# Attention scores: own PSUM banks and an own minimum for each component, and six banks in rotation ahead of attention

## The chip, the cores and the metric

The kernel runs on one core of one Trainium2 chip. The metric is the device time of one execution in microseconds, the median of three runs. [...]

## What is computed

One step of a hybrid trunk: a gated feed-forward half step, then a mixer of two branches (differential attention and a bidirectional mLSTM) whose outputs are gated by sigmoids and summed, then a second half step. 512 sample tokens and 128 prompt tokens are laid out as 640 columns. The part that matters here is the attention: 8 heads, each with two components c of 64 features, whose softmaxes are subtracted.

```python
s = einsum('bqhcd,bkhcd->bhcqk', q, k) * scale
pr = softmax(s, axis=-1)
w = pr[:, :, 0] - lam * pr[:, :, 1]
out = einsum('bhqk,bkhv->bqhv', w, v)
```

The stage ahead of it computes twelve 256-column slices of the input projection (`w_gd`, `w_gm`, `w_mo`, `w_mq`, `w_mk`), the branch gates among them.

## The kernel before

All matrix products are fp32 made of three products of a high part (`H`) and a low part (`L`); splitting a weight takes a copy on ScalarE (the high part) and a subtraction on VectorE (the low part). TensorE's instructions stand in the order in which the code is written. Those of ScalarE and VectorE are ordered by the framework's scheduler, except where the code pins them, so a change of what waits for what can move them.

The stages in time: FFN1 up to 466 us; from there to 505 us the second half of norm2, the projections of q and k of the first two heads (`tok_group`, L1220: two or three units of 128 tokens at a time, 8 steps k of 3 matmuls for each unit, then an evacuation by ScalarE into `q_tok` or `k_tok`) and the gate products `ps_g`; the gate items (`class Gates`, L1783, run by `Winograd.products`, L383 to L453) from 505 to 655 us; the preparation of head 0; attention from 684 to 1070 us; then mLSTM, the output and FFN2.

A gate item is one 1024 x 256 slice of weights in a Winograd scheme of seven products, each of 12 matmuls over 320 columns. It takes three PSUM tiles X, Y, Z (`acc_tile`, names `ps_f` in the profile). TensorE's order for item i is: A11 into X; ScalarE copies X to Y; S1 into Z; then the tail of item i-1 (A22 into its Y); S2 into Y, copied to SBUF as `u2` by ScalarE; the rest of the tail (S4 into the Z of item i-1, read by `done(1, 0, Z, u2)`); A12 into X, read by `done(0, 0, X, None)`; S3 into Y, copied as `u3`, and Z with u3 is read by `done(1, 1, Z, u3)`. A `done` writes a tile `g_out`, by VectorE where it adds a `u`, and stores it. Beside that ScalarE and VectorE split the weights of the coming items (`wB`, `wC` by `parts`, the sums `ww` by `sums`), and in items 1 to 5 they also normalise and rotate q and k (`rope`, `ss`, `q_tok`, `k_tok`). From item 5 on, VectorE also computes columns of the modulation (`junk,mod<-raw_a,csil`).

In attention each head has four blocks of 128 sample tokens with 768 keys and one block of 128 prompt tokens with 128 keys. Per block: `scores` (L1597) writes both components into one tile `sc` of three banks, VectorE takes the minimum of both (L1617; q is scaled by a negative number), `soft` makes the exponents of each component on ScalarE with that minimum as bias, `mix` combines them on VectorE, `turn` transposes the weights (`ps_wT`, copied to `wT` by ScalarE), and `values` multiplies by v (`ps_o`). Between these, `fill` puts matmuls of other projections (`ps_t`, `ps_p`), so that TensorE has work while the chain runs. All tiles but `sc` rotate through the five banks of the pool `ps2`, in the order in which the code asks for them.

```python
for c in range(2):
    if qi < 4:
        for k0, k1 in (((0, 512), (512, 768)) if c == 0 else ((0, 256), (256, 768))):
            o = s[:, c * 768 + k0 : c * 768 + k1]
...
placed(vec.tensor_reduce(out=mn, in_=sv, axis=AX.X, op=ALU.min))
```

Of the kernel before, what the change touches and what calls it, by code (L numbers as in the profile page):

```python
# [31 lines left out]
def tile_trunk(ctx: ExitStack, tc: tile.TileContext, a: dict):  # L32
# [4 lines left out]
    def placed(ins):  # L37
        if as_written[0] is in_row:
            i = ins.ins
            if i.engine in in_row:  # L40
                tc.add_manual_dep(
                    i, in_row[i.engine].name, mybir.DependencyInfo(mybir.DependencyClass.NoSync, mybir.DependencyReason.DATA),
                    reason="written",
                )
            in_row[i.engine] = i
        elif as_written[0]:
            tc.keep_in_program_order(ins)
        return ins

    def act(*args, **kw):  # L50
        return placed(nc.scalar.activation(*args, **kw))  # L51
# [22 lines left out]
    def mm(*args, **kw):  # L74
        tc.keep_in_program_order(nc.tensor.matmul(*args, **kw))  # L75
# [88 lines left out]
    class Banks:  # L164


        def __init__(self, pool):
            self.pool, self.order = pool, list(range(8))

        def tile(self, shape, dtype, tag, name):  # L170
            i = self.order.pop(0)
            self.order.append(i)
            return self.pool.tile(shape, dtype, tag=f"b{i}", name=name)
# [657 lines left out]
    with ExitStack() as ph:  # L831
# [514 lines left out]

    att = ExitStack()
    qk = att.enter_context(tc.tile_pool(name="qk", bufs=1))
    psum = att.enter_context(tc.tile_pool(name="ps2", bufs=5, space=PSUM))
    ps_s = att.enter_context(tc.tile_pool(name="ps2s", bufs=1, space=PSUM))  # L1350

    fill = Fill()


    def gate_products():
        raw = load(rawp, [128, KT, 128], a["w_g"], tag="raw", name="wg_raw")
        wgH = wide_p.tile([128, KT, 128], F32R, tag="BH", name="wgH", bufs=2)
        wgL = wide_p.tile([128, KT, 128], F32R, tag="BL", name="wgL", bufs=2)
        act(wgH, raw, AF.Copy)
        tt(vec, wgL, raw, wgH.bitcast(F32), ALU.subtract)  # L1360
        ps = ps_s.tile([128, 1536], F32, tag="sc", name="ps_g")

        def step(hf, k):
            cs = half(hf)
            mm3(ps[:, 512 * hf : 512 * hf + HALF], wgH[:, k, :], wgL[:, k, :], hH[:, k, cs], hL[:, k, cs], k == 0, k == KT - 1)

        return ps, step
# [175 lines left out]
    class Head:  # L1543
# [51 lines left out]
                self.turn_features(self.kp2, self.kL, True, lambda o, i: act(o, i, AF.Copy))  # L1595

        def scores(self, qi):  # L1597
            s = ps_s.tile([128, 1536], F32, tag="sc", name="sc")
            qs = slice(qi * 128, (qi + 1) * 128)
            qT, kH, kL = self.qT, self.kH, self.kL  # L1600
            for c in range(2):
                if qi < 4:
                    for k0, k1 in (((0, 512), (512, 768)) if c == 0 else ((0, 256), (256, 768))):
                        o = s[:, c * 768 + k0 : c * 768 + k1]
                        mm(o, qT[:, c, qs], kH[:, c, k0:k1], start=True, stop=False)
                        mm(o, qT[:, c, qs], kL[:, c, k0:k1], start=False, stop=True)
                else:

                    o = s[:, c * 512 : c * 512 + 256].rearrange("p (c t) -> p c t", c=2)
                    mm(o, qT[:, c, qs], kH[:, :, 768:896], start=True, stop=False)  # L1610
                    mm(o, qT[:, c, qs], kL[:, :, 768:896], start=False, stop=True)
            if qi < 4:
                sv = s.rearrange("p (c t) -> p c t", c=2)
            else:
                sv = s[:, 0:1280].rearrange("p (c t) -> p c t", c=2)[:, :, 0:128]
            mn, sm, rc = (ap.tile([128, 2], F32, tag=n, name=n, bufs=2) for n in ("mn", "sm", "rc"))
            placed(vec.tensor_reduce(out=mn, in_=sv, axis=AX.X, op=ALU.min))  # L1617
            self.s[qi] = sv, 768 if qi < 4 else 128, mn, sm, rc

        def soft(self, qi):  # L1620
            sv, w, mn, sm, rc = self.s[qi]
            p0 = ap.tile([128, 768], F32, tag="p0", name="p0", bufs=2)
            p1 = ap.tile([128, 768], F32, tag="p1", name="p1")
            for c, p in enumerate((p0, p1)):
                self.exp = act(p[:, :w], sv[:, c, :], AF.Exp, bias=mn[:, c : c + 1], scale=-1.0, accum_out=sm[:, c : c + 1])
            self.s[qi] = p0, p1, w, sm, rc

        def mix(self, qi):
# [201 lines left out]
    ropes, tabs, nlam, gs, rope_p = [], [], [None], [None], [None]  # L1830
    wide = ExitStack()
    wide_p = wide.enter_context(tc.tile_pool(name="wide", bufs=1))
    G = Gates(wide_p, ntmp, psum)

    (src_q, e_q), (src_k, e_k) = project_q(0, ropes.append), project_k(0, ropes.append)
    e_q, e_k = e_q(), e_k()
# [4 lines left out]

    def norm2_second(k):
        if k == 2:
            box["normed"] = norm2(psum, 1)

    tok_group(psum, [(w_q, 0, e_q), (w_q, 1, e_q)], norm2_second)
    tok_group(psum, [(w_k, 0, e_k), (w_k, 1, e_k)], lambda k: None)
    with tc.issue_after(box["normed"]):
        ps_g, gate_step = gate_products()

    heads = [Head(hd) for hd in range(8)]
    gates = ExitStack()
    tok_group(psum, [(w_q, i, e_q) for i in (2, 3, 4)], lambda k: None)
    G.work[0][0].load()
    with tc.issue_after(box["normed"]):
        third, fourth = G.operand_sums(lambda r: box["x"][1][:, 2 * r : 2 * r + 2, :])
        third()
        fourth()
    x_stack.close()
    tok_group(psum, [(w_k, i, e_k) for i in (2, 3, 4)], lambda k: None)  # L1860
    for k in range(KT):
        for hf in range(2):
            gate_step(hf, k)
# [702 lines left out]
```

## Time and profile before

| | us |
|---|---|
| median of 3 runs | 1814.83 (1814.38 to 1815.23) |
| profiled execution, its own time | 1815.7 |
| its span | 1813.9 |
| TensorE busy | 1785.6 (98%) |
| VectorE busy | 1349.6 (74%) |
| ScalarE busy | 910.8 (50%) |
| 466 to 505 us: TensorE busy | 37.6 of 39 |
| 505 to 655 us: TensorE busy | 148.4 of 150 |
| 655 to 684 us: TensorE busy | 29.0 of 29 |
| 684 to 1070 us: TensorE busy | 380.9 of 386 |

PE is TensorE's matmuls, PEld its weight loads, DVE VectorE, ACT ScalarE. In a row of the timeline the first number is the start in us from the span's start, the second the duration; then the engine, the line, the operation, the output and inputs by their names, the shapes, and in brackets the idle time ahead of it with what ended it. In a row of the waits stand the waiting engine and tile, what ended the wait, the total in us, the count and the longest. In a row of the windows stand, after the length, the busy time (and number of instructions) of PE, PEld, DVE, ACT and POOL, the granted clock, the DMA share and GB/s. L75 is the matmul helper, L51 the activation helper, L54 `tensor_tensor`, L57 `scalar_tensor_tensor`, L61 `tensor_scalar`: the tile's name tells which one it is.

### The profile page before, as it was taken

The page shows a single profiled execution, that of the slowest core. Times are in us where ns is not written, and L with a number is a line of the kernel's source. Part 1 is how long each engine was busy: PE and PEld are TensorE (multiplying, and loading weights), DVE is VectorE, ACT ScalarE, POOL GpSimd, SP SyncE. Part 2 cuts the span into 40 slices and gives each one's busy share as a digit, 9 for nine tenths or more (in the row PEclk, how much of TensorE's full clock was granted, in tenths as well). Part 3 has the DMA queues.
Part 4 walks back from the last instruction along what each step waited for, and adds up shares of the span by engine and source line. Part 5 has one row for each costly group of instructions (what it writes and reads, how often), then busy time and mean ns, then how long its engine had stood idle before and what let it go on. Part 6 is the DMA issues. An engine that isn't in the chain of part 4 may idle for free.

```text
span 1813.9 us, 30780 instructions
## 1 busy us (share of the span) xinstructions
PE 1785.6 (98%) x12550; PEld 1744.6 (96%) x12550; DVE 1349.6 (74%) x2178; ACT 910.8 (50%) x1588; POOL 39.2 (2%) x69
## 2 busy tenths in 40 slices
PE   8999999999999999999999999999999999999998
PEld 6999999999999999999999998899999999999998
DVE  6879987677888765858584557977767888897485
ACT  5654544333655445556564547674336545554432
POOL 0000000100000000000000000000000000000010
PEclk9999999999999999999999999999999999999999
DMA  8355566977245434221221124576642355557992
GB/s 326 111 198 171 186 236 221 350 227 266 83 139 181 160 131 143 78 69 63 69 69 55 68 81 163 182 257 218 221 171 80 134 173 185 203 180 274 353 311 80
DMA packets 132207, 311.36 MB, mean 172 GB/s; under 512 B 10017, under 2 KB 93217, under 8 KB 119009
## 3 DMA queue, kind: packets, MB, share of 16 engines
q1 hardware_dynamic: 121122, 265.22, 42.3%
q0 software_dynamic: 10256, 41.55, 7.1%
q8 instruction: 98, 1.61, 0.4%
q10 hardware_dynamic: 688, 2.63, 0.4%
q14 instruction: 43, 0.35, 0.1%
HBM read 240.49 MB, written 68.87 MB: 171 GB/s over the span
## 4 chain that ended last, share of the span: by engine, by line
PE 85%; DVE 7%; DMA 4%; ACT 2%; issue 1%; SPq 0%; DVEq 0%; ACTq 0%
PE ps_f L75 48%; PE ps_p L75 14%; PE ps_t L75 12%; PE sc L75 2%; PE ps_n L75 2%; PE ps_o L75 2%; DVE ww L54 2%; PE ps_u L75 1%; DMA raw_a<-in_w_ada_k 1%; PE ps_wT L78 1%; PE ps_qkT L78 1%; DMA raw<-in_w2b 1%; DVE junk L814 1%; DMA P<-nm_dram 1%; DVE mn L1617 1%
## 5 line engine op out<-in xcount | busy, mean ns | idle before, releaser
L75 PE MATMUL ps_f<-S,ww 128*128 128x320 f32 x2400 | 387.5, 310 | 5.2 <-DVE ww L54 1.9
L75 PEld LDWEIGHTS ps_f<-S,ww 128*128 128x128 f32 x2400 | 359.8, 188 | 9.6 <-DVE ww L54 6.5
L54 DVE TENSOR_TENSOR ww<-raw,ww 128x2048 fp32r<-128x2048 f32 (+1 forms) x73 | 163.9, 2246 | 74.3 <-ACT ww L51 74.2
L75 PE MATMUL ps_t<-wH,hH 128*128 128x256 f32 x640 | 185.7, 290 | 0.9 <-DVE x L57 0.9
L75 PE MATMUL ps_f<-hm,ww 128*128 128x320 f32 x1176 | 185.8, 309 | 0.1
L75 PE MATMUL ps_t<-wH,hL 128*128 128x256 f32 x640 | 181.6, 284 | 0.9 <-DVE hL L54 0.9
L75 PE MATMUL ps_t<-wL,hH 128*128 128x256 f32 x640 | 181.4, 283 | 0.0
L75 PEld LDWEIGHTS ps_f<-hm,ww 128*128 128x128 f32 x1176 | 175.7, 188 | 0.6 <-DVE ww L54 0.6
L51 ACT ACTIVATE ww<-raw 128x2048 fp32r<-128x2048 f32 (+1 forms) x73 | 136.9, 1875 | 60.3 <-DVE raw L54 33.0
L54 DVE TENSOR_TENSOR raw<-raw 128x1024 f32<-128x1024 f32 x186 | 161.0, 865 | 2.2
L75 PE MATMUL ps_f<-hm,wB 128*128 128x320 f32 x1008 | 161.5, 309 | 0.0
L75 PE MATMUL ps_p<-hH,wH 128*128 128x320 f32 x480 | 151.1, 315 | 0.7 <-ACT aT L51 0.7
L75 PEld LDWEIGHTS ps_f<-hm,wB 128*128 128x128 f32 x1008 | 151.3, 188 | 0.0
L75 PE MATMUL ps_p<-hH,wL 128*128 128x320 f32 x480 | 148.3, 309 | 0.0
L75 PE MATMUL ps_p<-hL,wH 128*128 128x320 f32 x480 | 148.3, 309 | 0.0
L51 ACT ACTIVATE u<-ps_f 128x320 f32<-128x320 f32 x129 | 55.8, 433 | 161.5 <-PE ps_f L75 159.7
L75 PEld LDWEIGHTS ps_t<-wH,hH 128*128 128x128 f32 x640 | 123.0, 192 | 1.5 <-ACT nsq L51 1.1
L75 PEld LDWEIGHTS ps_t<-wH,hL 128*128 128x128 f32 x640 | 122.9, 192 | 1.1 <-DVE hL L54 1.1
L75 PEld LDWEIGHTS ps_t<-wL,hH 128*128 128x128 f32 x640 | 123.1, 192 | 0.4
L1617 DVE TENSOR_REDUCE mn<-sc 128x2 f32<-128x1536 f32 (+1 forms) x40 | 59.5, 1489 | 56.0 <-PE sc L75 55.8
L54 DVE TENSOR_TENSOR wB<-raw,wB 128x1024 fp32r<-128x1024 f32 x64 | 78.1, 1221 | 26.7 <-ACT wB L51 26.7
L51 ACT ACTIVATE wH<-raw 128x2048 fp32r<-128x2048 f32 (+1 forms) x45 | 75.4, 1681 | 42.2 <-PE ps_p L75 35.5
(309 smaller groups left out, 3621.9 us busy)
## 6 DMA issues: line engine op xcount, KB each, us to landing
g_dram<-g SPq DMA_DIRECT2D x44, 640.0 KB, 7.6
raw_a<-in_w_ada_c POOLq DMA_DIRECT2D x35, 512.0 KB, 4.7
g_dram<-g SPq DMA_DIRECT2D x24, 480.0 KB, 8.1
raw<-in_w1b SPq DMA_DIRECT2D x11, 1024.0 KB, 4.9
raw<-in_w3b SPq DMA_DIRECT2D x11, 1024.0 KB, 6.3
raw<-in_w1a SPq DMA_DIRECT2D x10, 1024.0 KB, 4.9
raw<-in_w3a SPq DMA_DIRECT2D x10, 1024.0 KB, 6.2
hm<-g_dram SPq DMA_DIRECT2D x7, 1280.0 KB, 12.5
```

Of the source, the lines that this page charges most:

```text
L51: return placed(nc.scalar.activation(*args, **kw))
L54: return placed(eng.tensor_tensor(out=out, in0=in0, in1=in1, op=op))
L75: tc.keep_in_program_order(nc.tensor.matmul(*args, **kw))
L78: tc.keep_in_program_order(nc.tensor.transpose(*args, **kw))
L814: placed(vec.tensor_tensor_reduce(out=junk, in0=raw, in1=self.csil[:, v, :], op0=ALU.mult, op1=ALU.add, scale=1.0, scalar=0.0, accum_out=m ...
L1617: placed(vec.tensor_reduce(out=mn, in_=sv, axis=AX.X, op=ALU.min))
```

## The change

The ring `ps2` has four banks instead of five. The score tiles become two, tags `s0` and `s1`, of two banks each. In `scores` every component has its own tile, the larger piece (512 keys) always first, and its own minimum over 768 (or 128) columns; the exponent of a component reads that tile and that column of `mn`. Ahead of attention the two banks of `s1` serve as a fifth and sixth bank: the class `Six` hands out tiles in turn, four from the ring and then the two halves of one tile `more`. The projections `tok_group`, the second half of norm2 and the gate items take their tiles from it. `ps_g` lies in `s0`.

```diff
-    psum = att.enter_context(tc.tile_pool(name="ps2", bufs=5, space=PSUM))
+    psum = att.enter_context(tc.tile_pool(name="ps2", bufs=4, space=PSUM))
     ps_s = att.enter_context(tc.tile_pool(name="ps2s", bufs=1, space=PSUM))
+
+    class Six:
+
+
+        def __init__(self):
+            self.n, self.more = 0, ps_s.tile([128, 1024], F32, tag="s1", name="more")
+
+        def tile(self, shape, dtype, tag, name):
+            n, self.n = self.n % 6, self.n + 1
+            return psum.tile(shape, dtype, tag=tag, name=name) if n < 4 else self.more[:, 512 * n - 2048 : 512 * n - 1536]
+
+    six = Six()
...
-        ps = ps_s.tile([128, 1536], F32, tag="sc", name="ps_g")
+        ps = ps_s.tile([128, 1024], F32, tag="s0", name="ps_g")
...
         def scores(self, qi):
-            s = ps_s.tile([128, 1536], F32, tag="sc", name="sc")
             qs = slice(qi * 128, (qi + 1) * 128)
             qT, kH, kL = self.qT, self.kH, self.kL
+            mn, sm, rc = (ap.tile([128, 2], F32, tag=n, name=n, bufs=2) for n in ("mn", "sm", "rc"))
+            sv = []
             for c in range(2):
+                s = ps_s.tile([128, 1024], F32, tag=f"s{c}", name="sc")
                 if qi < 4:
-                    for k0, k1 in (((0, 512), (512, 768)) if c == 0 else ((0, 256), (256, 768))):
-                        o = s[:, c * 768 + k0 : c * 768 + k1]
-                        mm(o, qT[:, c, qs], kH[:, c, k0:k1], start=True, stop=False)
-                        mm(o, qT[:, c, qs], kL[:, c, k0:k1], start=False, stop=True)
+                    for k0, k1 in ((0, 512), (512, 768)):
+                        mm(s[:, k0:k1], qT[:, c, qs], kH[:, c, k0:k1], start=True, stop=False)
+                        mm(s[:, k0:k1], qT[:, c, qs], kL[:, c, k0:k1], start=False, stop=True)
+                    sv.append(s[:, 0:768])
                 else:
...
-            placed(vec.tensor_reduce(out=mn, in_=sv, axis=AX.X, op=ALU.min))
+                    sv.append(s[:, 128 * c : 128 * c + 128])
+                placed(vec.tensor_reduce(out=mn[:, c : c + 1], in_=sv[c], axis=AX.X, op=ALU.min))
...
-                self.exp = act(p[:, :w], sv[:, c, :], AF.Exp, bias=mn[:, c : c + 1], scale=-1.0, accum_out=sm[:, c : c + 1])
+                self.exp = act(p[:, :w], sv[c], AF.Exp, bias=mn[:, c : c + 1], scale=-1.0, accum_out=sm[:, c : c + 1])
...
-    G = Gates(wide_p, ntmp, psum)
+    G = Gates(wide_p, ntmp, six)
...
-    tok_group(psum, [(w_k, 0, e_k), (w_k, 1, e_k)], lambda k: None)
+    tok_group(six, [(w_k, 0, e_k), (w_k, 1, e_k)], lambda k: None)
...
-    tok_group(psum, [(w_q, i, e_q) for i in (2, 3, 4)], lambda k: None)
+    tok_group(six, [(w_q, i, e_q) for i in (2, 3, 4)], lambda k: None)
```

Besides the 40 reductions more on VectorE the instructions are the same, and TensorE has them in the same order. What they wait for differs, and ScalarE and VectorE are ordered anew. Three places follow.

TensorE at the end of item 1 and the start of item 2 of the gate items, with the engines that a row waits for. The rows `<-S,ww` are S3 of item 1, the rows `<-hH,wB` the first product A11 of item 2, written into its tile X. Before:

```order
L75 MATMUL ps_f<-S,ww 128x320 [waits Activation_49]
L75 MATMUL ps_f<-S,ww 128x320 x11
L75 MATMUL ps_f<-hH,wB 128x320
L75 MATMUL ps_f<-hL,wB 128x320
L75 MATMUL ps_f<-hH,wB 128x320 x2
```

The same place in the changed program, where X is the second half of `more`:

```order
L75 MATMUL ps_f<-S,ww 128x320 [waits Activation_49]
L75 MATMUL ps_f<-S,ww 128x320 x11
L75 MATMUL more<-hH,wB 128x320 [waits DVE_49]
L75 MATMUL more<-hL,wB 128x320
L75 MATMUL more<-hH,wB 128x320 x2
```

No matmul has moved; the first into `more` waits for VectorE, where no wait stood before. The instruction it waits for is the `g_out` that reads the Z of item 1 in the other half of `more`.

ScalarE in item 8 of the gate items, from the copy of X to Y (`ps_f<-ps_f`, then `ps_f<-more`) to the weight parts `wC`. `ww<-raw` is the high part of the weight sums of item 9, `g_out` an evacuation, `u` the copy u2. Before:

```order
L51 ACTIVATE ps_f<-ps_f 128x320
L51 ACTIVATE g_out<-ps_f 128x320
L51 ACTIVATE ww<-raw 128x2048
L51 ACTIVATE u<-ps_f 128x320
L51 ACTIVATE wC<-raw 128x512
```

The changed program:

```order
L51 ACTIVATE ps_f<-more 128x320
L51 ACTIVATE ww<-raw 128x2048
L51 ACTIVATE g_out<-ps_f 128x320
L51 ACTIVATE u<-ps_f 128x320
L51 ACTIVATE wC<-raw 128x512
```

`ww<-raw` has moved ahead of the evacuation `g_out`, which it followed.

VectorE in item 5 and at the start of item 6. `ww<-raw,ww` is the low part of the weight sums of item 6, `junk,mod` the modulation column, and the last row the `g_out` that reads the Z of item 5 with u3. Before:

```order
L54 TENSOR_TENSOR g_out<-ps_f,u 128x320
L54 TENSOR_TENSOR raw<-raw 128x4x128
L61 TENSOR_SCALAR g_out<-g_out 128x320
L814 ISA junk,mod<-raw_a,csil 128x1024
L814 ISA mod 128x1
L54 TENSOR_TENSOR ww<-raw,ww 128x2048
L54 TENSOR_TENSOR wB<-raw,wB 128x1024
L54 TENSOR_TENSOR wC<-raw,wC 128x512
L814 ISA junk,mod<-raw_a,csil 128x1024
L814 ISA mod 128x1
L57 SCALAR_TENSOR_TENSOR g_out<-ps_f,u 128x320
```

The changed program:

```order
L54 TENSOR_TENSOR ww<-raw,ww 128x2048
L54 TENSOR_TENSOR g_out<-ps_f,u 128x320
L814 ISA junk,mod<-raw_a,csil 128x1024
L814 ISA mod 128x1
L54 TENSOR_TENSOR wC<-raw,wC 128x512
L61 TENSOR_SCALAR g_out<-g_out 128x320
L814 ISA junk,mod<-raw_a,csil 128x1024
L814 ISA mod 128x1
L54 TENSOR_TENSOR wB<-raw,wB 128x1024
L57 SCALAR_TENSOR_TENSOR g_out<-more,u 128x320
```

`ww` now stands ahead of the first `junk,mod`, which it followed; the last `g_out` still comes after both `junk,mod` and the two weight parts.

More of the change, by code (lines that the diff above doesn't have):

```diff
@@ L1597, in scores @@
         def scores(self, qi):
-            s = ps_s.tile([128, 1536], F32, tag="sc", name="sc")
             qs = slice(qi * 128, (qi + 1) * 128)
             qT, kH, kL = self.qT, self.kH, self.kL
+            mn, sm, rc = (ap.tile([128, 2], F32, tag=n, name=n, bufs=2) for n in ("mn", "sm", "rc"))
+            sv = []
             for c in range(2):
+                s = ps_s.tile([128, 1024], F32, tag=f"s{c}", name="sc")
                 if qi < 4:
-                    for k0, k1 in (((0, 512), (512, 768)) if c == 0 else ((0, 256), (256, 768))):
-                        o = s[:, c * 768 + k0 : c * 768 + k1]
-                        mm(o, qT[:, c, qs], kH[:, c, k0:k1], start=True, stop=False)
-                        mm(o, qT[:, c, qs], kL[:, c, k0:k1], start=False, stop=True)
+                    for k0, k1 in ((0, 512), (512, 768)):
+                        mm(s[:, k0:k1], qT[:, c, qs], kH[:, c, k0:k1], start=True, stop=False)
+                        mm(s[:, k0:k1], qT[:, c, qs], kL[:, c, k0:k1], start=False, stop=True)
+                    sv.append(s[:, 0:768])
                 else:
-                    o = s[:, c * 512 : c * 512 + 256].rearrange("p (c t) -> p c t", c=2)
+                    o = s[:, 0:256].rearrange("p (c t) -> p c t", c=2)
                     mm(o, qT[:, c, qs], kH[:, :, 768:896], start=True, stop=False)
                     mm(o, qT[:, c, qs], kL[:, :, 768:896], start=False, stop=True)
[L1612 to L1617, printed above, removed]
+                    sv.append(s[:, 128 * c : 128 * c + 128])
+                placed(vec.tensor_reduce(out=mn[:, c : c + 1], in_=sv[c], axis=AX.X, op=ALU.min))
             self.s[qi] = sv, 768 if qi < 4 else 128, mn, sm, rc
@@ L1843, in norm2_second @@
         if k == 2:
-            box["normed"] = norm2(psum, 1)
-    tok_group(psum, [(w_q, 0, e_q), (w_q, 1, e_q)], norm2_second)
-    tok_group(psum, [(w_k, 0, e_k), (w_k, 1, e_k)], lambda k: None)
+            box["normed"] = norm2(six, 1)
+    tok_group(six, [(w_q, 0, e_q), (w_q, 1, e_q)], norm2_second)
+    tok_group(six, [(w_k, 0, e_k), (w_k, 1, e_k)], lambda k: None)
     with tc.issue_after(box["normed"]):
@@ L1859, in tile_trunk @@
     x_stack.close()
-    tok_group(psum, [(w_k, i, e_k) for i in (2, 3, 4)], lambda k: None)
+    tok_group(six, [(w_k, i, e_k) for i in (2, 3, 4)], lambda k: None)
     for k in range(KT):
```

## The prediction

> **What bounds the kernel now.** The page comes first: of 1813.9 us TensorE is busy for 1785.6, so a change can give back little and has to be judged by which waits of TensorE it takes away and which it adds.
>
> ```profile
> span 1813.9 us, 30780 instructions
> PE 1785.6 (98%) x12550; PEld 1744.6 (96%) x12550; DVE 1349.6 (74%) x2178; ACT 910.8 (50%) x1588; POOL 39.2 (2%) x69
> ```
>
> Then the busy time by stage, over the three stretches that the change touches: the first token projections with the second half of norm2, the twelve gate items, and attention.
>
> ```profile
> 466.00:505.00 39.00, 37.56 (x291) 36.52 (x292) 36.09 (x57) 25.53 (x48) 0.00 (x0) 1.00 0.20 67
> 505.00:655.00 150.00, 148.36 (x1012) 148.09 (x1011) 115.73 (x158) 73.56 (x113) 2.11 (x4) 1.00 0.49 167
> 684.00:1070.00 386.00, 380.85 (x3034) 370.82 (x3033) 250.91 (x385) 214.90 (x453) 0.00 (x0) 1.00 0.22 74
> ```
>
> The first number after each length is TensorE's busy time: it stands still for 1.4, 1.6 and 5.2 us. VectorE is full in the first stretch (36.1 of 39) and at 77% in the second. The waits of TensorE over 466 to 1070 us say what ends that idle time:
>
> ```profile
> PE ps_wT L78 <- DVE p L57: 3.0, 7, 0.8
> PE ps_f L75 <- DVE ww L54: 1.6, 1, 1.6
> PE sc L75 <- ACT p L51: 1.6, 3, 0.9
> PE ps_t L75 <- DVE hL L54: 0.9, 1, 0.9
> PE ps_o L75 <- ACT wT L51: 0.5, 1, 0.5
> ```
>
> The columns are the total, the count and the longest. In attention only three lines belong to the chain scores, minimum, exponent, mix, turn: 5.1 us in all. That is the most a shorter chain could give back.
>
> **The change part by part.**
>
> *The chain in attention.* Per block one reduction over both components becomes two over one each, and the exponent of component 0 no longer waits for component 1.
>
> ```profile
> L75 PE MATMUL sc<-kH,qT x144: 274/283/500, 683.8 to 1063.5; 128*128 128x256 f32 x80, 128*128 128x512 f32 x64
> L51 ACT ACTIVATE p<-sc,mn x80: 366/896/923, 687.9 to 1065.5; 128x768 f32<-128x768 f32 x64, 128x128 f32<-128x128 f32 x16
> L1617 DVE TENSOR_REDUCE mn<-sc x40: 417/1758/1760, 686.1 to 1063.9; 128x2 f32<-128x1536 f32 x32, 128x2 f32<-128x256 f32 x8
> ```
>
> From 417 ns at 256 columns and 1758 at 1536 a column costs 1.048 ns and the rest 149 ns; 768 columns are then 0.95 us (an estimate), two of them 1.91 against 1.76. VectorE gets 0.15 us more for each of 32 blocks, 4.8 us in all, in a stretch where it is idle for 135 of 386: I cost this at nothing. The first exponent starts about 1.5 us earlier (0.8 of the reduction, 0.7 of component 1's four matmuls: five gate products of 12 matmuls over 320 columns take 8.80 us, below, so 256 columns take 0.12 and 512 twice that; an estimate). Of the 5.1 us I take the three waits of scores on the exponents whole (1.6 us) and 0.9 of the 3.5 in front of the turn and the values: most of those follow VectorE's weight splits and ScalarE's rope copies, which stay. Gain 2.5 us, between 1 and 4.
>
> *Four banks instead of five in attention.* Every tile of the ring now needs the bank that was left four tiles before. I laid the tiles of the program's order on four banks and looked where the former tile's evacuation ends after TensorE gets there. Two examples:
>
> ```profile
> 754.59 0.39 PE L75 MATMUL ps_p<-hH,wH 128*128 128x320 f32 x1
> 755.51 0.59 ACT L51 ACTIVATE wT<-ps_wT 128x512 f32<-128x512 f32 x1
> 823.50 1.90 ACT L51 ACTIVATE wH<-raw 128x2048 fp32r<-128x2048 f32 x1
> 825.28 0.35 PE L75 MATMUL ps_t<-wH,hH 128*128 128x256 f32 x1
> 825.30 1.26 ACT L51 ACTIVATE rope<-k_tok 128x1280 f32<-128x1280 f32 x1
> 826.46 0.27 ACT L51 ACTIVATE wT<-ps_wT 128x128 f32<-128x128 f32 x1
> ```
>
> The matmul at 754.59 takes the bank whose wT copy ends at 756.10: 1.5 us. The one at 825.28 waits for 826.73: 1.45 us, and a second wait of 0.2 follows within its head. Ahead of both copies ScalarE has a 1.9 us weight copy and a 1.3 us rope copy, in the same order in the changed program, so this isn't given back. The second place comes again one pair of heads later (1.65), and four places of 0.1 to 0.5 add about 1. Sum 5.8 us; nothing at best, where ScalarE reaches the copies sooner, 6.8 at worst.
>
> *The first projections.* The extra two banks are one tile, `more`. Both halves have one owner for the framework, so a write to one half waits for a read of the other. The third group of projections (w_q, units 2 to 4) is the first to write the second half; the first half still holds a result of the group before, the second k_tok copy.
>
> ```profile
> 479.71 0.28 PE L75 MATMUL ps_t<-wH,hH 128*128 128x256 f32 x1
> 481.03 0.39 PE L75 MATMUL ps_t<-wH,hL 128*128 128x256 f32 x1 [0.92 <-DVE hL L54]
> 484.49 0.37 ACT L51 ACTIVATE k_tok<-ps_t 128x256 f32<-128x256 f32 x1
> ```
>
> ScalarE gets to that copy only after the hH rows of norm2, at 484.86. TensorE, there at 479.71, would stand for 5.15 us. The 0.92 us that it now waits for hL two matmuls later falls away behind it: 4.2 net. The same happens once more in the next group (its third unit writes the first half while q_tok is read from the second); ScalarE has moved that copy behind sums that VectorE delivers, I take 0.6 (0 to 1). Together +4.8 us.
>
> *The gate items.* Each item has three tiles X, Y, Z and seven products of 12 matmuls. With six tiles in rotation the items 0, 2, 4, 6, 8, 10 have X in the second half of `more`, the odd ones Z in the first. So in each even item from 2 on, the first product into X (A11) waits for the g_out that reads the former Z with u3, and A12 into X for the g_out that reads it with u2: ten waits that were not there (the order of TensorE above shows the first). Item 8, where the work is regular:
>
> ```profile
> 595.46 1.92 ACT L51 ACTIVATE ww<-raw 128x2048 fp32r<-128x2048 f32 x1 [1.20 <-PE ps_f L75]
> 597.41 2.29 DVE L54 TENSOR_TENSOR ww<-raw,ww 128x2048 fp32r<-128x2048 f32 x1 [1.31 <-ACT ww L51]
> 602.45 0.31 PE L75 MATMUL ps_f<-hH,wB 128*128 128x320 f32 x1
> 602.65 0.44 ACT L51 ACTIVATE u<-ps_f 128x320 f32<-128x320 f32 x1 [0.52 <-PE ps_f L75]
> 604.28 0.49 DVE L54 TENSOR_TENSOR g_out<-ps_f,u 128x320 f32<-128x320 f32 x1
> 608.31 1.90 ACT L51 ACTIVATE ww<-raw 128x2048 fp32r<-128x2048 f32 x1
> 611.25 0.31 PE L75 MATMUL ps_f<-hH,wB 128*128 128x320 f32 x1
> 612.46 0.49 DVE L54 TENSOR_TENSOR g_out<-ps_f,u 128x320 f32<-128x320 f32 x1
> ```
>
> A11 is due at 602.45, g_out ends at 604.77: 2.3 us. A later TensorE doesn't shrink this: VectorE works without a break from 597.41, started by a copy that TensorE itself releases at 595.46. A12 is due at 611.25, g_out ends at 612.95: 1.7. Here the new order lets ScalarE's ww go ahead of a copy that it followed. An item lasts 12.32 us (526.63 to 575.91 below is four of them), so item 7 began at 590.13, its ww went 5.33 after, and item 8's could go at 607.78, not 608.31: 0.5 less, 1.2 us. Items 8 and 10: 3.5 each.
>
> [...]
>
> The other even items, by A11 and the g_out that it will wait for:
>
> ```profile
> 526.63 0.31 PE L75 MATMUL ps_f<-hH,wB 128*128 128x320 f32 x1
> 528.95 0.49 DVE L54 TENSOR_TENSOR g_out<-ps_f,u 128x320 f32<-128x320 f32 x1
> 538.03 0.48 DVE L54 TENSOR_TENSOR g_out<-ps_f,u 128x320 f32<-128x320 f32 x1
> 551.27 0.31 PE L75 MATMUL ps_f<-hH,wB 128*128 128x320 f32 x1
> 555.37 0.48 DVE L54 TENSOR_TENSOR g_out<-ps_f,u 128x320 f32<-128x320 f32 x1
> 560.62 0.48 DVE L54 TENSOR_TENSOR g_out<-ps_f,u 128x320 f32<-128x320 f32 x1
> 575.91 0.31 PE L75 MATMUL ps_f<-hH,wB 128*128 128x320 f32 x1
> 577.42 2.29 DVE L54 TENSOR_TENSOR ww<-raw,ww 128x2048 fp32r<-128x2048 f32 x1 [1.39 <-ACT ww L51]
> 582.51 0.49 DVE L57 SCALAR_TENSOR_TENSOR g_out<-ps_f,u 128x320 f32<-128x320 f32 x1
> ```
>
> A12 stands 8.80 us after A11 (602.45 to 611.25). Item 2: 2.8 and 3.1 by these rows; VectorE's ww now stands ahead of a g_out that waits for TensorE (0.8 less at A11), and ScalarE's ww goes 0.5 sooner: 4.6. Item 4: 4.6 and 1.0, 5.6; the rope steps are moved ahead of its first g_out and away from the second, which I take to balance. Item 6: 7.1 by the row, but only because ww came late (577.42). In the new order ww, g_out and the rest stand as in item 8, so 2.3 + 1.2 = 3.5. Sum 4.6 + 5.6 + 3 x 3.5 = 20.7 us. With the late ww goes the 1.6 us wait on it: -1.6.
>
> The ends for these ten: by the rows as they are, 27.3; and at least what no order can avoid. After the product before A11 comes u (602.65 + 0.44) and then g_out (0.49): 1.1 us. After the one before A12 comes g_out alone: 0.7. That is 5 x 1.8 = 9.
>
> *Everything else*, FFN1, mLSTM, the output and FFN2, keeps its banks and its order.
>
> The sum: 4.8 + 20.7 - 1.6 + 5.8 - 2.5 = +27.2 us. The profiled execution took 1815.7 us (its span and 1.8 around it), which gives 1842.9; the median of before, 1814.83, lies 0.9 lower, so 1842.0.
>
> **The rivals.**
>
> A. VectorE catches up. While TensorE stands, VectorE and ScalarE work off what is queued, and each wait falls to its floor: 9 instead of 20.7, giving 1830. For it: both have idle time in the stage. Against: in item 8 VectorE's run starts from TensorE, not from a backlog.
>
> B. Nothing is gained by the new order and every wait costs what the rows of before say: 27.3, and 6.8 for the banks, with 4.8 of the projections, 1.6 of ww still paid and 1 gained in attention: +37.9, or 1852.7. For it: VectorE has the rope steps of q and k on top in items 2 to 5. Against: the order did move.
>
> C. Not slower: the two halves are guarded apart, so A11 follows its predecessor at the usual pitch. Then the terms of the projections and gate items are nothing, 1.6 of ww comes back, and if the wT copies on ScalarE come early enough for four banks, the attention chain gives its 2.5: -4.1, 1810.7. It decides at the first A11 of item 2: a wait for g_out there ends it. [...] Against: the order shows that wait.
>
> D. The same, but the four banks cost their 5.8: +1.7, 1816.5, which is within 0.2% (3.6 us, about what a measurement of this kernel can tell from no change).
>
> **How the numbers follow.** The waits on `more` are in the program, not a guess, so the forecast and its neighbours A and B hold nearly everything: forecast 0.66, A 0.18, B 0.09, C 0.03, D 0.04. The range runs from 1829 to 1850: it takes in A and most of the way to B; C, D and the far end of B are left out. Faster 0.03, same 0.04, slower 0.93.
>
> **What would show it.** In the changed profile, TensorE's waits must have a new line, ps_f or `more` waiting for DVE g_out, ten times and about 20 us; one of some 5 us near 479.7 for ScalarE's k_tok; no wait for ww near 578; in attention fewer waits of sc on ACT p, and new ones of ps_p and ps_t on ACT wT near the two places above. The two reductions of a block should take 0.95 us each. The forecast is wrong if the g_out waits are missing or under 1 us each, if the stage of gate items is not some 19 us longer, or if attention has grown by over 7 us or shrunk.

## The result and the profile after

The changed kernel takes 1847.35 us (median of four executions, 1846.86 to 1850.12), the kernel before 1815.03 (four, 1814.38 to 1817.99). The ratio is 1.0178 (95% interval 1.016 to 1.0196), or 32 us more. The profiled execution took 1846.86 us, 31.2 more than that of before.

Where they lie is read first from the score matmuls, which begin and end attention. The rows of the changed kernel (count, shortest, median and longest duration in ns, first and last start in us):

```profile
L75 PE MATMUL sc<-kH,qT x144: 276/308/477, 714.8 to 1094.6; 128*128 128x256 f32 x80, 128*128 128x512 f32 x64
L1627 DVE TENSOR_REDUCE mn<-sc x80: 278/948/959, 716.5 to 1095.1; 128x1 f32<-128x768 f32 x64, 128x1 f32<-128x128 f32 x16
```

Attention starts at 714.8 instead of 683.8, 31.0 us later, and lasts 379.8 us as before (379.7). So the whole difference lies ahead of it. The windows of before, from the end of FFN1 to the first score:

```profile
466.00:684.00 218.00, 214.92 (x1550) 213.57 (x1550) 174.28 (x251) 113.46 (x187) 2.11 (x4) 1.00 0.42 144
```

The same stretch of the changed kernel, and its attention:

```profile
466.00:715.00 249.00, 224.97 (x1549) 221.06 (x1550) 175.55 (x252) 115.07 (x186) 2.10 (x4) 0.97 0.37 126
...
715.00:1101.00 386.00, 379.46 (x3033) 371.06 (x3033) 254.92 (x424) 214.76 (x453) 0.00 (x0) 1.00 0.22 74
```

The stretch is 31.0 us longer. TensorE's idle time in it goes from 3.1 us (218 less 214.92) to 24.0 (249 less 224.97): 20.9 of the 31. The other 10.1 is busy time: the same matmuls keep TensorE busy for longer, and the granted clock has fallen from 1.00 to 0.97. Which waits make the idle time is in the waits of TensorE from 466 to 690 us (total, count, longest):

```profile
PE more L75 <- DVE g_out L54: 14.8, 8, 2.5
PE more L75 <- ACT k_tok L51: 5.0, 1, 5.0
PE more L75 <- DVE g_out L57: 3.3, 2, 2.2
```

Eleven waits, all of the tile `more`: ten for `g_out`, 18.1 us together, and one of 5.0 for `k_tok`. The 1.6 us for `ww` and the 0.9 for hL are gone: 23.1 - 2.5 = 20.6. The eleven one by one, from the timeline (start, duration, and in brackets the idle time ahead):

```profile
484.67 0.39 PE L75 MATMUL more<-wH,hH 128*128 128x256 f32 x1 [5.02 <-ACT k_tok L51]
533.65 0.42 PE L75 MATMUL more<-hH,wB 128*128 128x320 f32 x1 [1.49 <-DVE g_out L54]
545.18 0.41 PE L75 MATMUL more<-hH,wB 128*128 128x320 f32 x1 [2.46 <-DVE g_out L54]
564.80 0.41 PE L75 MATMUL more<-hH,wB 128*128 128x320 f32 x1 [1.99 <-DVE g_out L54]
576.23 0.41 PE L75 MATMUL more<-hH,wB 128*128 128x320 f32 x1 [2.36 <-DVE g_out L54]
596.06 0.41 PE L75 MATMUL more<-hH,wB 128*128 128x320 f32 x1 [2.21 <-DVE g_out L57]
607.72 0.42 PE L75 MATMUL more<-hH,wB 128*128 128x320 f32 x1 [1.06 <-DVE g_out L57]
626.03 0.41 PE L75 MATMUL more<-hH,wB 128*128 128x320 f32 x1 [2.21 <-DVE g_out L54]
636.15 0.41 PE L75 MATMUL more<-hH,wB 128*128 128x320 f32 x1 [1.06 <-DVE g_out L54]
654.46 0.42 PE L75 MATMUL more<-hH,wB 128*128 128x320 f32 x1 [2.20 <-DVE g_out L54]
666.12 0.42 PE L75 MATMUL more<-hH,wB 128*128 128x320 f32 x1 [1.06 <-DVE g_out L54]
```

The pairs are A11 and A12 of the items 2, 4, 6, 8 and 10, five even items as forecast. Items 6, 8 and 10 are alike to 0.01 us. The chain behind the pair of item 8, in the same timeline:

```profile
616.67 1.92 ACT L51 ACTIVATE ww<-raw 128x2048 fp32r<-128x2048 f32 x1 [2.24 <-PE ps_f L75]
618.62 2.29 DVE L54 TENSOR_TENSOR ww<-raw,ww 128x2048 fp32r<-128x2048 f32 x1 [1.31 <-ACT ww L51]
...
625.49 0.48 DVE L54 TENSOR_TENSOR g_out<-more,u 128x320 f32<-128x320 f32 x1
...
633.41 2.29 DVE L54 TENSOR_TENSOR ww<-raw,ww 128x2048 fp32r<-128x2048 f32 x1 [4.85 <-ACT ww L51]
635.62 0.48 DVE L54 TENSOR_TENSOR g_out<-more,u 128x320 f32<-128x320 f32 x1
```

TensorE releases ScalarE's `ww` at 616.67, that releases VectorE's, and `g_out` stands behind it: it ends at 625.97, and A11 starts at 626.03. In attention the waits of TensorE (710 to 1100 us) are other ones than before, with a total of 6.5 us instead of 5.1:

```profile
PE ps_t L75 <- ACT wT L51: 2.7, 2, 1.3
PE ps_wT L78 <- DVE p L57: 1.6, 3, 1.1
PE ps_p L75 <- ACT wT L51: 1.3, 1, 1.3
PE ps_o L75 <- ACT wT L51: 0.5, 1, 0.5
PE sc L75 <- ACT kL L51: 0.4, 1, 0.4
```

The waits of `ps_t` and `ps_p` on `wT` are those of a ring of four. That of the scores on the exponents, 1.6 us before, is gone, and that of the turn on VectorE has gone from 3.0 to 1.6.

### The profile page after: what moved, and what is told of

Its sections match the earlier page's. It is cut to its first block, busy times and chain, and to the rows that moved or that the text cites. A ratio compares the mean times of both kernels' runs of the same rounds, so it can differ in the third digit from the quotient of the medians.

```text
span 1845.1 us, 30876 instructions
## 1 busy us (share of the span) xinstructions
PE 1794.7 (97%) x12550; PEld 1753.8 (95%) x12550; DVE 1354.3 (73%) x2218; ACT 912.2 (49%) x1588; POOL 39.2 (2%) x69
## 4 chain that ended last, share of the span: by engine, by line
PE 82%; DVE 7%; DMA 4%; ACT 4%; issue 2%; SPq 0%; DVEq 0%; ACTq 0%
PE ps_f L75 43%; PE ps_p L75 15%; PE ps_t L75 11%; PE sc L75 3%; PE more L75 2%; PE ps_o L75 2%; DVE ww L54 2%; PE ps_n L75 2%; DMA raw_a<-in_w_ada_k 1%; DVE junk L814 1%; PE ps_wT L78 1%; PE ps_u L75 1%; ACT ww L51 1%; PE ps_qkT L78 1%; DMA raw<-in_w2b 1%
## 5 line engine op out<-in xcount | busy, mean ns | idle before, releaser
L75 PE MATMUL ps_f<-S,ww 128*128 128x320 f32 x2328 | 379.6, 312 | 3.5 <-DMA S<-g_dram 1.0
L75 PEld LDWEIGHTS ps_f<-S,ww 128*128 128x128 f32 x2328 | 353.5, 190 | 7.4 <-DVE ww L54 4.6
L75 PE MATMUL ps_t<-wH,hH 128*128 128x256 f32 x616 | 179.3, 291 | 4.0 <-ACT wT L51 2.7
L75 PE MATMUL ps_t<-wL,hH 128*128 128x256 f32 x616 | 174.8, 284 | 0.0
L75 PE MATMUL ps_t<-wH,hL 128*128 128x256 f32 x616 | 174.8, 284 | 0.0
L75 PEld LDWEIGHTS ps_t<-wH,hH 128*128 128x128 f32 x616 | 118.4, 192 | 5.4 <-ACT wT L51 2.9
L75 PEld LDWEIGHTS ps_t<-wL,hH 128*128 128x128 f32 x616 | 118.6, 193 | 0.1
L75 PEld LDWEIGHTS ps_t<-wH,hL 128*128 128x128 f32 x616 | 118.5, 192 | 0.0
L1627 DVE TENSOR_REDUCE mn<-sc 128x1 f32<-128x768 f32 (+1 forms) x80 | 62.4, 818 | 52.7 <-PE sc L75 52.7
```

Of the source, the lines that this page charges most:

```text
L1627: placed(vec.tensor_reduce(out=mn[:, c : c + 1], in_=sv[c], axis=AX.X, op=ALU.min))
```

## The experiments

The theory: the two extra banks are halves of one tile, 512 of its 1024 columns each, so each half waits for readers of the other. Its rivals: the rotation over six banks itself, the new order on VectorE and ScalarE, or the four banks in attention cost the time. What opened on the way is the lowered clock, and what the two halves of the change in attention are worth by themselves. Spans below are those of one profiled execution each; ratios are to the kernel before on the same chip.

### The two banks as two tiles

```diff
-            return psum.tile(shape, dtype, tag=tag, name=name) if n < 4 else self.more[:, 512 * n - 2048 : 512 * n - 1536]
...
+            if n < 4:
+                return psum.tile(shape, dtype, tag=tag, name=name)
...
+            return self.pool.tile([128, 512], F32, tag=f"x{n}", name=name)
...
+    six = Six(True, 6)
...
+    six.stack.close()
+    ps_s[1] = att.enter_context(tc.tile_pool(name="ps2t", bufs=1, space=PSUM))
```

The pool of the two extra tiles is closed ahead of attention, and the score tile `s1` gets its banks then. In `Six(True, 6)` the first argument asks for two tiles (`False` for the common one), the second is the number of banks that rotate.

> The changed kernel with one edit: the two extra banks ahead of attention are two tiles, each with its own buffer, instead of the two halves of one tile. The same six banks rotate in the same order, and attention is as in the changed kernel. If the shared owner of the halves is the cause: no wait on g_out ahead of an A11 or A12, none on k_tok near 480 us, no lowered clock in the gate stage, the first score matmul at 682 to 685 us instead of 714.8, and 1811 to 1817 us in all. If the cause is the rotation over six banks, the new order on ScalarE and VectorE, or the four banks in attention: at least 1835 us remain.

Measured: 1817.25 us, ratio 1.0007 (0.9998 to 1.0017), span 1812.7 against 1845.1. Its waits of TensorE from 466 to 690 us:

```profile
PE ps_f L75 <- DVE ww L54: 1.8, 1, 1.8
PE ps_t L75 <- DVE hL L54: 0.9, 1, 0.9
```

No wait for `g_out` or `k_tok` is left, the two old ones are back, and the granted clock is 1.00 throughout the stage. Attention starts at 683.2 us. The rotation over six banks is the same as in the changed kernel, and so are the score tiles: the loss comes with the common tile. At the two places whose order was shown ahead of the prediction, ScalarE and VectorE have the order of before again: in item 8 ScalarE's `g_out` starts at 606.73 and `ww` behind it at 607.74, in item 5 VectorE's first `junk,mod` at 574.12 and `ww` at 576.16. So the new order comes with the common tile, and what it costs or saves by itself is not shown; that TensorE stands for readers of the other half is read from the eleven waits above. The banks are the same as in the changed kernel and the eleven waits (23.1 us) are not there: what set them was the common tile.

### Five banks instead of six

```diff
-    six = Six(True, 6)
+    six = Six(True, 5)
```

On top of the two tiles; the sixth bank isn't used.

> As the kernel with two tiles, but only five banks rotate ahead of attention, as before the change (one bank idle); attention as in the changed kernel. If the shared owner is the cause, this equals the kernel with two tiles within 2 us, and the sixth bank by itself is worth nothing or up to 1.6 us (the wait for ww in item 6). If the rotation over six is the cause, this one is near 1815 us and the one with two tiles stays over 1835.

Measured: 1815.6 us, ratio 1.0007 (0.9998 to 1.0016), span 1812.7, attention from 683.0 to 1062.8. The sixth bank is worth nothing here, 1.0007 with five as with six: in the kernel before, TensorE's waits from 469 to 684 us were 1.6 us for `ww`, 0.9 for hL and 0.4 for `nsq`, all of them inputs of its matmuls, so there was nothing to give.

### Only the projections, or only the gate items, share a tile

```diff
     tok_group(six, [(w_k, i, e_k) for i in (2, 3, 4)], lambda k: None)
+    six.stack.close()
+    six = Six(True, 6)
+    G.psum = six
```

Here the projections have the common tile (`Six(False, 6)` further up) and the gate items get two. The second kernel has them the other way round.

> Only the projections and norm2 ahead of the gate items share one tile; the gate items have two separate tiles. If the waits add up by place: 5.0 us of wait on k_tok come, 0.9 of hL go, and one stretch of about 3.5 us at a lower clock costs 1.7: 4 to 6 us above the kernel with two tiles, no wait on g_out. If a later TensorE only lets VectorE catch up, the difference shrinks to under 2 us by the end.

> Only the gate items share one tile; the projections have two separate ones. If the waits add up by place: ten waits on g_out, 17 to 20 us together, no wait for ww in item 6 (-1.6), and three or four stretches at a lower clock (1.7 us each): 21 to 27 us above the kernel with two tiles. If most of the time lost in the gate stage came from the late start that the projections cause, under 12 us.

Measured, projections alone: 1823.73 us, ratio 1.0046 (1.0028 to 1.0064), span 9.0 us over that with two tiles: more than expected. Its wait and the windows behind it (the granted clock is the number after the last bracket):

```profile
PE more L75 <- ACT k_tok L51: 5.0, 1, 5.0
```

```profile
484.00:488.00 4.00, 3.95 (x18) 3.96 (x19) 3.96 (x7) 0.59 (x1) 0.00 (x0) 0.50 0.15 23
488.00:492.00 4.00, 4.00 (x30) 4.00 (x29) 4.00 (x6) 1.89 (x4) 0.00 (x0) 0.81 0.60 244
```

Attention starts 6.9 us later (690.1 against 683.2). The wait gives 5.0, the hL wait that goes 0.9 back, and the clock costs the rest: 3.95 us at 0.50 and 4.00 at 0.81 lose 2.7. The other 2.1 of the 9.0 lie behind attention. In mLSTM a wait of `ps_u` for ScalarE's `Cn` took 2.1 us, with two tiles 1.6, and behind it a lowered clock (0.72 from 1126 to 1130 us, 0.85 from 1130 to 1134) cost 1.2 more; that leaves 0.4 without a name.

Gate items alone: 1842.41 us, ratio 1.0150 (1.0134 to 1.0167), span 28.1 us over two tiles. Its waits from 466 to 690 us:

```profile
PE more L75 <- DVE g_out L54: 16.2, 8, 2.7
PE more L75 <- DVE g_out L57: 3.3, 2, 2.2
```

19.5 us of waits less the 1.8 for `ww`, which is gone, are 17.7; attention starts 27.4 us later, four stretches of lowered clock (0.58, 0.74, 0.68 and 0.64 in the lowest window of 4 us of each) make 6.2 of the difference, and 3.5 are left without a name. The longest wait of this run, 2.70 us at A11 of item 2, isn't among the four that such a stretch follows. Its row in the timeline and the window behind it:

```profile
529.30 0.42 PE L75 MATMUL more<-hH,wB 128*128 128x320 f32 x1 [2.70 <-DVE g_out L54]
530.00:532.00 2.00, 2.00 (x16) 2.00 (x15) 2.00 (x6) 0.42 (x1) 0.00 (x0) 1.00 0.57 212
```

The two parts give 6.9 and 27.4 us, together 2.7 more than both at once (714.8 - 683.2 = 31.6): after the projections' wait the gate items wait 1.4 less (A11 of items 2 and 4: 1.49 and 1.99 us instead of 2.70 and 2.10).

### The other phase of the rotation

```diff
+    six = Six(False, 6)
+    G.psum = six
+    turn_of[0] = 4
```

The gate items alone share, but the rotation starts at the fifth tile, so that the two halves are X and Y of one even item instead of the Z of one item and the X of the next.

> As the kernel in which only the gate items share one tile, with the rotation shifted by one: the halves of the shared tile are now X and Y of the same even item, no longer the Z of one item and the X of the next. If the cost is set by which product follows directly on a read of the other half: the ten waits of A11 and A12 on the Z's g_out are gone; S3 into Y of each even item follows A12 and waits for the read of X, 0.6 to 1.5 us, six times; together 4 to 9 us, no lowered clock, 1819 to 1826 us. If the sharing as such costs the same wherever the halves lie: near 1842 us.

Measured: 1828.25 us, ratio 1.0088 (1.0074 to 1.0102), span 13.4 us over two tiles. That is half of the 28.1 of the same kernel in the other phase, so it matters which tiles share; but it is more than expected, by one wait that I had not seen. Two of the rows of its waits from 466 to 690 us, and that wait in the timeline:

```profile
PE more L75 <- DVE g_out L61: 6.6, 4, 4.3
PE more L75 <- ACT g_out L51: 2.7, 2, 1.3
...
569.62 3.57 PE L75 MATMUL more<-S,ww 128*128 128x320 f32 x12 [4.30 <-DVE g_out L61]
```

S3 into Y waits for the scaled `g_out` that reads X, and that stands on VectorE behind `ww`, `wC` and steps of `rope` and `k_tok`. Behind it, from 570 to 574 us, the clock is at 0.50.

### The ring of four by itself

The kernel before, with four banks in attention only (five ahead of it), one score tile of three banks and the common minimum.

```diff
-    psum = att.enter_context(tc.tile_pool(name="ps2", bufs=5, space=PSUM))
+    psum = att.enter_context(tc.tile_pool(name="ps2", bufs=4, space=PSUM))
...
+            return (psum if n < 4 else self.pool).tile(shape, dtype, tag=tag, name=name)
...
+    five.stack.close()
```

> The kernel before with one edit: the ring has four banks in attention instead of five (ahead of attention five rotate as before, the fifth from a pool of its own). Scores keep their one tile of three banks and the common minimum. If four banks cost what the changed profile shows at three places (1.5 us each) and some small ones: attention 4 to 6 us longer than before, waits of ps_p and ps_t on ACT wT, 1819 to 1821 us; and the own minima then gave back the difference to the kernel with two tiles, 4 to 6 us. If four banks cost nothing and the own minima gave nothing: 1815 us.

Measured: 1823.79 us, ratio 1.0057 (1.0043 to 1.0071). The row of its scores and its waits of TensorE from 720 to 1095 us:

```profile
L75 PE MATMUL sc<-kH,qT x144: 277/283/499, 683.1 to 1068.9; 128*128 128x256 f32 x80, 128*128 128x512 f32 x64
```

```profile
PE ps_wT L78 <- DVE p L57: 3.3, 6, 0.9
PE ps_t L75 <- ACT wT L51: 2.7, 2, 1.3
PE sc L75 <- ACT p L51: 1.6, 3, 0.9
PE ps_p L75 <- ACT wT L51: 1.3, 1, 1.3
PE ps_p L75 <- ACT aT L51: 0.9, 1, 0.9
```

Attention lasts 385.8 us instead of 379.7: the bank costs 6 us, mostly by the waits on `wT` that the prediction named. From this kernel to the one with five banks rotating, attention goes from 385.8 to 379.8 us; the only difference there is the two score tiles with their own minima, the larger piece first in each. They give the same 6 us back. By the medians both are larger, 10 us (ratio 1.0057 to before) and 9 (1.0057 to 1.0007), so each size is known to some 4 us only. That the two cancel holds by either measure.

### Idle matmuls in the waits

Does the lowered clock cost time by itself? These kernels are the changed one with matmuls of 192 columns into free columns of `ps_g` ahead of the waits, whose products nothing reads, so that TensorE isn't idle there.

```diff
+                if hasattr(self, "warm") and i and i % 2 == 0:
+                    for _ in range(12):
+                        mm(self.warm[:, 320:512], gr.w[A11][0][0], A(A11)[:, 0, 0][:, 0:192], ...)
                 into(X, A11, True)
```

The second kernel has 48 of them ahead of the third projection group, 20 ahead of A11 and 8 ahead of A12.

> The changed kernel with 12 idle matmuls of 192 columns ahead of A11 in items 2, 4, 6, 8 and 10, in the time in which TensorE waits for g_out (their result is not used). If the stretches at a lower clock come from TensorE standing still: the waits on g_out at A11 shrink to about 1 us, the gate stage keeps its full clock except after the 5 us wait on k_tok, and 3 to 7 us are gained: 1840 to 1844 us. If the lower clock has another cause: no gain, and up to 6 us more, should the idle matmuls take longer than the waits.

> The changed kernel with idle matmuls of 192 columns in all eleven waits on the shared tile: 48 ahead of the third group of projections, 20 ahead of A11 and 8 ahead of A12 in items 2 to 10 (their result is not used). If the lowered clock follows from TensorE standing still: no stretch below full clock from 466 us to attention, the first score matmul at 705 to 708 us instead of 714.8, 1837 to 1841 us. If not: the lowered stretches stay, and the time stays at 1845 or more.

Measured with 12 ahead of A11: 1842.98 us, ratio 1.0163 (1.0149 to 1.0177), span 1839.6, 5.5 less than the changed kernel's. Its waits from 466 to 690 us:

```profile
PE more L75 <- DVE g_out L54: 9.2, 8, 2.5
PE more L75 <- ACT k_tok L51: 5.0, 1, 5.0
PE more L75 <- DVE g_out L57: 2.0, 2, 1.1
```

The filled waits fall, the unfilled one of 5.0 stays, and the clock is lowered only behind that one (0.50 from 484 to 488 us) and once more near 566. That second stretch stands behind a wait of 1.61 us, a filled one (its row in the timeline and a window behind it):

```profile
564.61 0.42 PE L75 MATMUL more<-hH,wB 128*128 128x320 f32 x1 [1.61 <-DVE g_out L54]
566.00:568.00 2.00, 2.00 (x9) 2.00 (x9) 1.97 (x5) 0.10 (x1) 0.00 (x0) 0.50 0.22 76
```

The unfilled wait of 2.46 at A12 of item 2 is as long as in the changed kernel, but here the clock stays up behind it (1.00 from 544 to 548 us and from 548 to 552). With all eleven filled: 1841.99 us, ratio 1.0150 (1.0136 to 1.0165), span 1840.7. The window behind the second wait of item 2, where the changed kernel had lost most:

```profile
546.00:550.00 4.00, 4.00 (x30) 4.00 (x29) 3.36 (x8) 3.02 (x6) 0.00 (x0) 1.00 0.67 266
```

In every window of 4 us from 466 us to attention the granted clock is 1.00. Attention starts at 710.3 instead of 714.8, a gain of 4.5 where I expected 7 to 10. Two things show in the timelines. This execution was already 1.2 us later ahead of the first idle matmul (the last matmul into `more` ahead of them is at 480.37, in the changed kernel at 479.13). And a full clock doesn't help where VectorE's `g_out` sets the time: A11 of item 4 starts at 564.85, in the changed kernel at 564.80, though TensorE had lost 1.7 us by the clock ahead of it there and none here. The ratio's interval just overlaps that of the changed kernel (1.0136 to 1.0165 against 1.016 to 1.0196), so the gain rests on the profiles more than on the medians. It is a test, not a cure: the waits stay.

### Taking the bank waits of attention away

Three attempts to make the kernel with two tiles faster than before. The first copies the shorter `wT` piece by VectorE; the second writes and issues the `rope` steps behind the next `wT` copy, which they stood ahead of on ScalarE; the third adds to the second the move of one modulation column from gate item 5 to 6, against the wait for `ww`.

```diff
-                act(wT[:, k0 : k0 + n, :], p[:, :n, :], AF.Copy)
+                (act(wT[...], p[...], AF.Copy) if n == 4 else placed(vec.tensor_copy(wT[...], p[...])))
```

```diff
-    def project_q(pr, now=lambda f: f()):
+    def project_q(pr, now=lambda f: late_ropes.append(f)):
...
+            with tc.issue_after(copied.ins):
+                while late_ropes:
+                    late_ropes.pop(0)()
```

```diff
-    IN_GATES = [(i, 1) for i in (5, 7, 9, 11)]
+    IN_GATES = [(i, 1) for i in (6, 7, 9, 11)]
```

> The kernel with two tiles, with one edit: the second, shorter piece of wT in each block (two of six key tiles, or the one of the prompt block) is copied by VectorE, not by ScalarE. If the three waits of 1.5 us for a bank come from ScalarE's queue (weight copy and rope copy ahead of the wT copy), they go: attention 3 to 5 us shorter, 1809 to 1812 us. If VectorE's own queue (weight splits of 2.3 us) delays the copies as much, nothing is gained or up to 5 us lost.

> The kernel with two tiles, with one edit: in attention the norm and rope of a projected q or k is written, and issued on ScalarE, behind the next copy of wT instead of ahead of it (1.26 us of rope copy out of the way; the 1.9 us weight copy stays). If ScalarE's queue is what the three waits for a bank come from: they fall from 1.3-1.5 to about 0.3 us each, attention gets 3 to 4 us shorter, 1811 to 1813 us in a comparison in which before has 1815. If the bank isn't released by that copy: no change.

> The kernel before this one, and the first column of the modulation moved from gate item 5 to item 6, so that VectorE doesn't wait for its data ahead of the ww of item 6: the wait of 1.6 to 1.8 us for ww in item 6 goes, 1.5 us less than the kernel before this one, if no other wait takes its place; 1809 to 1812 us.

Measured: 1817.22 us, ratio 1.0020 (1.0012 to 1.0029); 1820.16, ratio 1.0031 (1.0021 to 1.0041); 1821.14, ratio 1.0036 (1.0023 to 1.0048). None gains. In the first, attention lasts 379.7 us, as with two tiles (379.8): `ps_t` no longer waits for `wT`, but now 3.1 us for `ao`, VectorE's read of `ps_o`. In the second it lasts 383.0, where 3 to 4 us less were expected. The second one's waits from 684 to 1070 us:

```profile
PE ps_wT L78 <- DVE p L57: 3.7, 3, 2.4
PE ps_t L75 <- DVE ao L61: 2.4, 2, 1.2
...
PE ps_t L75 <- ACT wT L51: 0.4, 2, 0.2
```

The wait of `ps_t` for `wT` has fallen from 2.7 to 0.4, as meant, and the next reader of the same ring takes its place: `ao`, VectorE's read of `ps_o`, 2.4. One of the waits of the turn is now 2.4 long, and the clock falls behind it (0.57 from 778 to 782 us). In the third the `ww` wait stayed at 1.8: `ww` follows ScalarE's copy, not the modulation column. No version beat the kernel before.

## Why the prediction was right, and where it was not

The forecast was 1842.0 in a range of 1829 to 1850; 1847.35 lies inside, 5.4 above the forecast, by the mechanism forecast. The profiled execution took 31.2 us longer, where the sum said 27.2. By its terms:

- **Gate items**, forecast 20.7: 18.1 by the waits, ten of them. Items 6, 8 and 10 give 3.27 each (forecast 3.5), item 2 gives 3.95 (4.6), item 4 gives 4.35 (5.6). In item 4 the assumption that the moved `rope` steps balance was off by 1.25 us in the sum and by more at each place: 4.6 and 1.0 were forecast, 1.99 and 2.36 came. Rival A, that VectorE catches up, falls: item 8's chain starts from TensorE, as argued against it. A little of it is seen early on, the 1.4 us by which the gate items wait less behind the projections' wait.
- **Projections**, forecast 4.8: the wait was 5.02 (forecast 5.15) and took the hL wait of 0.92 with it. The second wait, 0.6, didn't come. 4.1 in all.
- **The `ww` wait**, forecast -1.6: gone. The run with two tiles has it again (1.8), but with the old order, so it doesn't tell whether the new order or the new waits took it away. That `junk,mod` stood ahead of `ww` was not what made it in the kernel with two tiles: with the column moved to item 6 it stayed at 1.8.
- **Four banks in attention**, forecast +5.8: 6.1 between the stages of the profiles, at the places named.
- **Own minima**, forecast -2.5 (1 to 4): -6.0. The reduction itself is as estimated, 0.948 us against 0.95. The size of the gain was wrong, and the step that failed is to put the most that a shorter chain could give at 5.1 us, the idle time in front of it, and to take half. From the kernel with the ring of four alone to the one with five banks rotating ahead of attention, TensorE's idle time in attention falls by 3.6 us (from 9.46 to 5.87), of which the listed waits give 3.3: the scores' 1.6 and 1.7 of the turn's 3.3. (The 0.9 of `ps_p` on `aT` comes behind the last scores and stays.) The other 2.4 is recorded busy time (376.34 to 373.93, both at a granted clock of 1.00), which a ceiling of idle time can't hold. Before has 375.22, or 373.6 without the loss by the clock that is named next, so this busy time came with the ring of four and went with the own minima. Why is open, and no run has the own minima with five banks in attention. Together attention came out at +0.1, where the sum had +3.3. One part of that is no effect of the change: before had a low clock of its own there, here in its windows, which costs it 1.7 us (4.86 us at 0.66) and which neither the changed kernel nor those with five banks rotating or with the ring of four alone had. Against a kernel without it the bank would have cost 7.8, by this estimate.

```profile
960.00:965.00 5.00, 4.86 (x28) 4.87 (x29) 2.75 (x8) 2.54 (x8) 0.00 (x0) 0.66 0.00 0
```

- **What the sum didn't have**: the clock. It costed a wait at its own length, but the granted clock fell behind five of the eleven, here behind that of 545.18:

```profile
546.00:550.00 4.00, 4.00 (x19) 4.00 (x18) 3.39 (x6) 2.73 (x6) 0.00 (x0) 0.57 0.56 215
550.00:554.00 4.00, 4.00 (x30) 4.00 (x28) 4.00 (x6) 1.78 (x3) 0.00 (x0) 1.00 0.07 23
```

19 matmuls in 4 us instead of 30. Over all windows of 4 us from 466 to 715, the busy time times the missing part of the clock sums to 7.6 us: a quarter of the loss. Of the 10.1 us of added busy time 2.5 remain. The first matmul after a wait is recorded with 0.42 instead of 0.31 us, which is 1.1 for ten of them; for the last 1.4 I have no name.

So the mechanism and its largest term were right; that the total came within 4 us is partly luck, because the clock (+7.6) and the rest of the busy time (+2.5), which the sum lacked, were partly met by attention (-3.2 against the forecast) and by idle time that came out at 20.9 instead of 23.9 (-3.0), errors that have nothing to do with each other. Rivals C and D, guarded halves, did not happen in the changed kernel, but the kernel with two tiles is what they describe: 1.0007 is +1.3 us, near the +1.7 of D. That is D's number and not its terms: D has +3.3 for attention and -1.6 for `ww`, while the profile of two tiles has +0.1 for attention (379.8 to 379.7) and still waits for `ww`.

## What to carry to other kernels

A tile that spans two banks is one tile to whoever places the semaphores: here that was eleven waits, 23.1 us, where two tiles had none of them. Before its halves are handed out as buffers of their own, look at who reads the one half while the other is written, or make two tiles of them. Look for a wait for a bank in the stage before a bank is added (here none was seen, and the sixth gave nothing: 1.0007 with it and without it); a bank less is costed by laying the tiles of the program's order on the ring and looking at the queue of the engine that reads each (5.8 us forecast, 6.1 measured). Cost a new wait of TensorE of 2 us or so at up to 1.7 times its length, as came out here (2.46 us of wait and 1.7 by the clock), since a stretch at a lowered clock may stand behind it, as behind five of the eleven; and when one wait of a ring is taken away, look which reader is late next (`wT` from 2.7 to 0.4 us, and 2.4 for `ao`).

## What the hardware showed

In the changed kernel the granted clock fell behind waits of 2.20, 2.21, 2.36, 2.46 and 5.02 us, but not behind another of 2.21 (626.03), nor behind any of 1.99 or less; each stretch cost 1.3 to 1.7 us (the busy time times the missing part of the clock), behind the longest wait 1.3. Behind the same wait of 5.0 it cost 2.7 in the kernel where the projections alone share.

The length of the wait alone doesn't decide. With the gate items alone sharing, the clock stayed up behind 2.70 us (1.00 from 530 to 532 us); with 12 idle matmuls it fell behind 1.61 (0.50 from 566 to 568) and stayed up behind 2.46 (1.00 from 544 to 552). In before, the low clock at 960 us (0.66 from there to 965) has two waits of 0.9 and 0.8 us ahead of it, 1.5 us apart, and none longer. What decides stays open; the runs show only that with matmuls in all eleven waits the granted clock is 1.00 in every window of 4 us from 466 us to attention.
